# The start of a decoder-trunk kernel written as a table of single steps

## Chip, cores and metric

One core of a Trainium2 chip runs the whole program in one launch. The metric is the time of an execution on the device in microseconds, lower is better. Engines are called as in the profile: PE (TensorE matmuls; PEld its weight loads), DVE (VectorE), ACT (ScalarE), POOL (GpSimd) and SP (the queue that issues most DMAs).

## What is computed

One layer of a hybrid decoder over 1024 prompt tokens and 64 new tokens (1088 columns), width 1024, in float32:

```python
h = rmsnorm(x, g_mix)
z = jnp.einsum('btd,dc->btc', h, w_in)                       # 1024 -> 5 * 512
b_gate, c_gate, v, glu_val, glu_gate = jnp.split(z, 5, axis=-1)
conv_a, new_a = causal_dwconv(c_gate * v, hist_a, conv_a_w)  # 3 taps
y_a = b_gate * conv_a
u_b = glu_val * jax.nn.sigmoid(glu_gate)
conv_b, new_b = causal_dwconv(u_b, hist_b, conv_b_w)         # 31 taps
y_b = jax.nn.silu(layernorm(conv_b + conv_b_bias, ln_b_g, ln_b_b))
x = x + jnp.einsum('btc,cd->btd', jnp.concatenate([y_a, y_b], axis=-1), w_out)
h2 = rmsnorm(x, g_ffn)
f = jax.nn.silu(h2 @ w_gate) * (h2 @ w_up)
x = x + f @ w_down                                           # then a last rmsnorm
```

## The kernel before

Channels lie on the 128 partitions, tokens along the free axis. Every product of two float32 matrices is made of float16 matrices: a value is split into a high half (rounded to float16) and a low half (what is left), and `products` (L217) multiplies high by high, high by low and low by high. So a block of 128 output rows over 8 blocks of the 1024 inputs is 24 matmuls per column range.

The change is in the **first phase**, which makes the norm and the first 4 of the 20 output blocks of the input projection (two gates and two values). There x comes in five chunks of columns (`FIRST`, L57): chunk 0 has 128 columns, chunk 1 has 144, chunks 2, 3 and 4 have 272. For a chunk s and a block k of 128 channels:

- squares: ACT (for half of chunk 0 DVE) squares x, four blocks at a time (`first_squares`, L594);
- halvings: DVE adds the eight blocks of squares in pairs, to one block for chunk 0 and to four for the others (`first_halves`, L605);
- column sums: PE multiplies what is left by a matrix of ones, in float32, and so adds over the partitions (`column_sums`, L251, matmul at L264, output `stat`); the profile counts two rows for each of these matmuls;
- the reciprocal root: two ACT functions and three DVE steps (`rstd_steps`, L271 to L281), the result again in `stat`;
- for each k: DVE multiplies x by the gain and the root into a tile `s` (L637), ACT rounds it to the high half (`high`, L246), DVE subtracts to get the low half (`low`, L249). The low half comes `LAG` = 3 blocks after its tile;
- products: 24 matmuls at L233 for the chunk and an output block, into a PSUM bank `one`.

The four weight blocks are split likewise: high half on ACT (L209), low half on DVE (L210). Gate blocks leave PSUM through a sigmoid on ACT (L667), value blocks through a product on DVE (L514) into the tiles `u` that the 31-tap convolution reads.

The Python text of L681 to L735 is a hand-written order of whole jobs: a chunk's norm, then a block's 24 products, then a chunk's sums, and so on. Each engine executes its instructions strictly in the order in which the text issues them, and waits where an operand isn't ready. So the order of the text is the order of each engine's queue. Among these jobs stand three calls of `fill` (L445), which split the first eight pieces of the weights of the next phase (`raws` 0 and 1); these weights are first scaled on POOL (L196), rounded on ACT (L207) and their low halves made on POOL (L208). `prepare` (L378) loads the next raw block ahead of its use.

After the first phase come the **convolution phase** (from 77.84 us: the other 16 blocks on PE, while DVE runs the 31 taps, L529 and L534), the output projection, and the gated network with a seven-product scheme; DVE makes most of their low halves.

The loads are issued by SP in the order of L310: x chunk 0, weight block 0, x 1, w 1, x 2, w 2, x 3, w 3, x 4.

## Time and profile before

| what | value |
| --- | --- |
| median of 3 runs | 1031.65 us (1030.02 to 1032.03) |
| the profiled execution's own time | 1029.85 us |
| its span, from first to last instruction | 1027.6 us |
| PE busy | 990.8 us (96%) |
| DVE busy | 764.4 us (74%) |
| ACT busy | 390.3 us (38%) |
| POOL busy | 322.6 us (31%) |

The time of the profiled execution holds the span and some 2.3 us around it. A busy share is an average over stages. How much a stage is worth is seen from where PE waits within it: the timeline of an engine lists its instructions in order of time, merged where they are alike, each with its start, the time that the group took, and in brackets the engine's idle time before it with what ended that idle time. A group of matmuls is counted with the pipeline's latency of its last one.

### The profile page before, as it was taken

The numbers are of one execution on the slowest core, as the hardware profiler recorded it, in microseconds if no ns is written. First come the engines' busy times: TensorE is split into PE (matmuls) and PEld (weight loads), VectorE is DVE, ScalarE is ACT, GpSimd is POOL, SyncE is SP. The second block draws the span as 40 slices with busy tenths as digits, with TensorE's granted clock in tenths as the row PEclk, the third lists the DMA queues.
The fourth block names the chain that finished last, engine by engine and source line by source line (L and its number), as shares of the span: only waits on it lengthen the run. The fifth ranks groups of instructions, "written<-read, shape, count | busy, mean of one in ns | idle before, by whom it ended". The sixth has DMA issues, their size and how long they took to land.

```text
span 1027.6 us, 19663 instructions
## 1 busy us (share of the span) xinstructions
PE 990.8 (96%) x8498; PEld 831.2 (81%) x8498; DVE 764.4 (74%) x1083; ACT 390.3 (38%) x694; POOL 322.6 (31%) x259
## 2 busy tenths in 40 slices
PE   4799999999999999999999999999999999999995
PEld 3688888887788878888888888888888888888884
DVE  6839999997687787887776668777676777665548
ACT  6541232335663434444322434332243433233332
POOL 0148764554200013421333332313332322240033
PEclk9899999999999999999999999999999999999998
DMA  9011111211320110111122112011211202111104
GB/s 346 27 42 42 42 42 42 94 42 43 134 83 1 42 42 6 77 42 60 36 72 83 42 41 73 32 35 70 83 42 42 72 32 63 62 63 42 42 1 175
DMA packets 17031, 63.02 MB, mean 61 GB/s; under 512 B 1168, under 2 KB 8480, under 8 KB 12080
## 3 DMA queue, kind: packets, MB, share of 16 engines
q1 hardware_dynamic: 16896, 61.67, 17.3%
q8 instruction: 66, 1.08, 0.4%
q14 instruction: 21, 0.17, 0.1%
q0 software_dynamic: 48, 0.09, 0.0%
HBM read 56.71 MB, written 5.05 MB: 60 GB/s over the span
## 4 chain that ended last, share of the span: by engine, by line
PE 67%; DVE 26%; ACT 3%; issue 2%; DMA 0%; DVEq 0%; ACTq 0%
PE two L233 63%; DVE cv L534 12%; PE one L233 3%; DVE xt L1378 1%; DVE whl L210 1%; DVE u L249 1%; DVE s L637 1%; DVE v L1010 1%; DVE s L281 1%; PE stat L258 1%; DVE h L249 1%; DVE s L280 1%; DVE u L610 1%; DVE cv L529 1%; DVE xt L1326 0%
## 5 line engine op out<-in xcount | busy, mean ns | idle before, releaser
L233 PEld LDWEIGHTS <-whl 128*128 128x128 f16 x7464 | 729.3, 98 | 141.3 <-issue 4.8
L233 PE MATMUL two<-u,whl 128*128 128x272 f16 x4416 | 523.7, 280 | 3.8 <-DVE u L249 2.8
L233 PE MATMUL two<-h,whl 128*128 128x272 f16 x1512 | 186.1, 280 | 0.0
L233 PE MATMUL two<-v,whl 128*128 128x272 f16 x1536 | 178.6, 279 | 0.1
L409 POOL TENSOR_TENSOR s<-wf,s 128x512 f32<-128x512 f32 (+1 forms) x32 | 46.9, 1465 | 383.1 <-DVE whl L210 383.1
L209 ACT ACTIVATE whl<-wf 128x512 f16<-128x512 f32 (+1 forms) x150 | 87.6, 589 | 143.0 <-PE two L233 141.3
L534 DVE SCALAR_TENSOR_TENSOR cv<-u,par_t,cv 128x1024 f32<-128x1024 f32 x116 | 139.7, 1280 | 0.0
L210 DVE SCALAR_TENSOR_TENSOR whl<-wf,whl 128x512 f16<-128x512 f32 (+1 forms) x150 | 108.9, 742 | 1.2 <-ACT whl L209 1.2
L1285 DVE SCALAR_TENSOR_TENSOR xt<-two,xt 128x544 f32<-128x544 f32 x108 | 75.8, 720 | 42.9 <-PE two L233 42.3
L1176 DVE SCALAR_TENSOR_TENSOR s<-two,s 128x544 f32<-128x544 f32 x40 | 28.9, 723 | 66.1 <-PE two L233 66.1
L209 ACT ACTIVATE whl<-s 128x512 f16<-128x512 f32 (+1 forms) x96 | 55.4, 583 | 59.5 <-PE two L233 57.4
L398 POOL TENSOR_TENSOR s<-wf 128x512 f32<-128x512 f32 (+1 forms) x32 | 40.9, 1278 | 108.9 <-DVE u L249 96.3
L210 DVE SCALAR_TENSOR_TENSOR whl<-s,whl 128x512 f16<-128x512 f32 (+1 forms) x96 | 66.6, 708 | 0.0
L208 POOL TENSOR_TENSOR whl<-wf,whl 128x512 f16<-128x512 f32 x38 | 44.1, 1182 | 41.3 <-ACT whl L207 41.3
L233 PE MATMUL two<-u,v 128*128 128x272 f16 x480 | 56.3, 279 | 0.7 <-DVE xt L949 0.7
L233 PEld LDWEIGHTS <-v 128*128 128x128 f16 x480 | 46.9, 98 | 10.0 <-issue 0.9
L246 ACT ACTIVATE h<-s 128x544 f16<-128x544 f32 x52 | 34.0, 657 | 52.8 <-DVE s L1169 48.2
L233 PE MATMUL one<-v,u 128*128 128x272 f16 (+2 forms) x480 | 47.5, 259 | 4.0 <-ACT v L246 2.4
L233 PEld LDWEIGHTS <-u 128*128 128x128 f16 x480 | 40.6, 99 | 11.4 <-issue 5.6
L1210 DVE SCALAR_TENSOR_TENSOR s<-two,s 128x544 f32<-128x544 f32 x20 | 14.5, 724 | 45.2 <-PE two L233 45.2
L405 POOL TENSOR_TENSOR wf<-wf 128x512 f32<-128x512 f32 (+1 forms) x32 | 46.6, 1457 | 0.0
L399 POOL TENSOR_TENSOR s<-s,wf 128x512 f32<-128x512 f32 (+1 forms) x32 | 41.9, 1309 | 2.5
(124 smaller groups left out, 750.9 us busy)
## 6 DMA issues: line engine op xcount, KB each, us to landing
wf<-w_gu SPq DMA_DIRECT2D x22, 1024.0 KB, 4.9
wf<-w_ds SPq DMA_DIRECT2D x12, 768.0 KB, 4.2
wf<-w_in SPq DMA_DIRECT2D x8, 1024.0 KB, 5.0
wf<-w_o SPq DMA_DIRECT2D x6, 1024.0 KB, 4.8
xt<-x SPq DMA_DIRECT2D x3, 1088.0 KB, 10.2
y<-xt SPq DMA_DIRECT2D x2, 1088.0 KB, 4.2
u<-w_in SPq DMA_DIRECT2D x4, 512.0 KB, 8.7
wf<-w_dl SPq DMA_DIRECT2D x2, 1024.0 KB, 5.0
```

The lines of the kernel that those rows point to most:

```text
L208: return whl, lambda: gps.tensor_tensor(lo, wf, hi, ALU.subtract) and None
L209: act.activation(hi, wf, AF.Copy, scale=WSC)
L210: return whl, lambda: dve.scalar_tensor_tensor(lo, wf, WSC, hi, ALU.mult, ALU.subtract) and None
L233: pe.matmul(out, w_[:, wpart, col : col + P], hl[:, apart, t0 : t0 + out.shape[1]], start=first and (i, q) == one, stop=last and (i, q) == ...
L246: act.activation(hi, tmp, AF.Copy)
L398: gps.tensor_tensor(s1, a21, a22, ALU.add)
L399: gps.tensor_tensor(s2, s1, a11, ALU.subtract)
L405: gps.tensor_tensor(a21, a11, a21, ALU.subtract)
L409: gps.tensor_tensor(src, a12, src, ALU.subtract)
L534: dve.scalar_tensor_tensor(o_, i_, w, c, ALU.mult, ALU.add)
L1176: dve.scalar_tensor_tensor(o, src, IN_SC, other, ALU.mult, ALU.add)
L1285: dve.scalar_tensor_tensor(o, bk[a_][:, :, :CW], IN_SC, o, ALU.mult, ALU.add)
```

## The change

The order of the first phase is now a table, `STARTUP`, of single steps; a loop walks it and issues each step. Letters name the step, then come the chunk and the block or part:

- SQ squares; HV a halving on DVE and HP one on POOL; ST one of the matmuls with ones;
- RY and RM the two ACT functions of the root, N its three DVE steps;
- T the normalised tile, HI its high half, LO its low half on DVE, LP its low half on POOL;
- WH and WL a weight block's halves; M half a block's products (12 of 24 matmuls);
- SG the sigmoid, V the product of gate and value;
- FS scaling of the next phase's raw weights, FH and FL the halves of its pieces.

Beside the order, four things differ. Chunks 1 to 4 are halved once more, to two blocks, so that two matmuls with ones are left for each where there were four. Of these eight halvings five stand on POOL (HP10, HP11, HP21, HP40, HP41) and three on DVE (HV20, HV30, HV31); before there were four, all on DVE. Of the 40 low halves 15 stand on POOL. The load of weight block 2 is issued ahead of x's chunk 2. `prepare` no longer loads the raw block 2 of the next phase; it is loaded and scaled at the end of the first phase. The number of products is the same.

```diff
-LAG = 3
+STARTUP = """
+SQ00 SQ01 HV00 WH0 HV01 HV02 ST00 WL0 RY0 RM0 SQ11 N00 N01 SQ10 N02 T06 WH1 HP10 T00 T04 T02
+HI06 T03 HI00 T01 HP11 HI02 T05 HI04 HI03 WL1 HI01 ST10 WH2 ST11 T07 LP00 LO03 LO02 RM1 LO04 RY1
...
+M32h0 FL4 M30h1 SG20 FL1 M31h1 FL6 M33h0 FL3 M23h0 M32h1 SG21 M33h1 V21 V20 M23h1 V11
+"""
 
...
-        ("x", 0), ("w", 0), ("x", 1), ("w", 1), ("x", 2), ("w", 2), ("x", 3), ("w", 3), ("x", 4)
+        ("x", 0), ("w", 0), ("x", 1), ("w", 1), ("w", 2), ("x", 2), ("w", 3), ("x", 3), ("x", 4)
...
-        for q in (r, r + 1):
+        for q in (r, r + 1) if r > 1 else (r,):
...
+    w4, low_w, accs = {}, {}, {}
+    squares_of, left, stat_of, r_of, of_k = {}, {}, {}, {}, {}
+    scaled.update(range(3))
...
+    def first_half(s, level, eng):
+
+        two = squares_of[s, 0]
+        n = 4 >> level
+        other = two[:, n : 2 * n] if level else squares_of.pop((s, 1))
+        eng.tensor_tensor(two[:, :n], two[:, :n], other, ALU.add)
+        left[s] = n
+
+    def first_stat(s, k):
+
+        if k == 0:
+            stat_of[s] = stat_banks()[:, 0, : FIRST[s][1]]
+        n = left[s]
+        pe.matmul(stat_of[s], ones, squares_of[s, 0][:, k], start=k == 0, stop=k == n - 1)
+        if k == n - 1:
+            squares_of.pop((s, 0))
+
...
+        if which == "y":
+            act.activation(
+                y0, st, AF.Abs_reciprocal_sqrt, bias=epst[:, 0:1], scale=1.0 / D
+            )
+        elif which == "m":
+            act.activation(m, st, AF.Identity, bias=epst[:, 0:1], scale=1.0 / D)
...
+    def first_norm(s, k, part):
+
+        hk = h[k][:, :, chunk(s)]
+        if part == "T":
+            t = of_k[s, k] = small()[:, : FIRST[s][1]]
+            dve.scalar_tensor_tensor(
+                t, xt[:, k, chunk(s)], prm(PG1 + k), stat_of[s], ALU.mult, ALU.mult
+            )
+        elif part == "HI":
+            high(hk[:, 0], of_k[s, k])
+        else:
+            low(hk[:, 1], of_k.pop((s, k)), hk[:, 0], gps if part == "LP" else dve)
+
+    def first_task(s, i, part):
         t0, cw = FIRST[s]
         c, o = t0 // CW, t0 % CW
+        if o == 0 and part == 0:
+            accs[c, i] = bank()
+        products(
+            [accs[c, i][:, o : o + cw]],
+            [(w4[i], k * P, [(h[k], t0)]) for k in range(KB)],
+            low_last=s == 0,
+            part=(12 * part, 12 * part + 12),
+        )
...
+    def first_step(step):
+
+        kind = step.rstrip("0123456789h")
+        d = [int(c) for c in step[len(kind) :] if c != "h"]
...
+        elif kind == "WH":
+            w4[d[0]], low_w[d[0]] = split_w(w4f[d[0]], resident=unit)
+        elif kind == "WL":
+            low_w.pop(d[0])()
...
+        elif kind == "FS":
+            r = d[0]
+            if r not in loaded:
+                loaded[r] = load_w(*raws[r][:2])
+            scale_w(loaded[r])
+        elif kind == "FH":
+            fill_one(0)
+            low_w["f", d[0]] = late.pop()
+        elif kind == "FL":
+            low_w.pop(("f", d[0]))()
+
+    keep = {}
+    for step in STARTUP.split():
+        first_step(step)
+    loaded[2] = load_w(*raws[2][:2])
+    scale_w(loaded[2])
```

The queue of POOL at its first tensor work. Before (`wf` a raw weight block, `whl` the halves of its pieces):

```order
L196 TENSOR_SCALAR wf_675<-wf_675 128x2048
L196 TENSOR_SCALAR wf_677<-wf_677 128x2048
L208 TENSOR_TENSOR whl_680<-wf_675,whl_680 128x512
L208 TENSOR_TENSOR whl_683<-wf_675,whl_683 128x512
L208 TENSOR_TENSOR whl_790<-wf_675,whl_790 128x512
L208 TENSOR_TENSOR whl_792<-wf_675,whl_792 128x512
```

With the change (`u` squares, `v` the halves of the normalised x, `s` the normalised tiles; L627 is a halving, L263 a low half):

```order
L627 TENSOR_TENSOR u_138<-u_138,u_134 128x576
L627 TENSOR_TENSOR u_138<-u_138 128x288
L263 TENSOR_TENSOR v_101<-s_146,v_101 128x128
L263 TENSOR_TENSOR v_108<-s_171,v_108 128x128
L263 TENSOR_TENSOR v_103<-s_206,v_103 128x144
L627 TENSOR_TENSOR u_204<-u_204 128x544
L263 TENSOR_TENSOR v_101<-s_251,v_101 128x144
L263 TENSOR_TENSOR v_102<-s_273,v_102 128x144
L627 TENSOR_TENSOR u_381<-u_381,u_352 128x1088
L627 TENSOR_TENSOR u_381<-u_381 128x544
L210 TENSOR_SCALAR wf_524<-wf_524 128x2048
```

Two halvings of chunk 1 now head the queue, and ten steps of the norm stand ahead of the first scaling.

The queue of PE at its start. Before (`stat` column sums, `one` an output block; `v_101` to `v_108` are the blocks k = 0 to 7 of the normalised x):

```order
L264 MATMUL stat_129<-u_119,ones 128x128
L233 LDWEIGHTS u_126
L233 MATMUL one_176<-v_101,u_126 128x128
...
L233 MATMUL one_176<-v_106,u_126 128x128
L264 MATMUL stat_189<-u_134,ones 128x144 x4
L233 LDWEIGHTS u_126
L233 MATMUL one_176<-v_107,u_126 128x128
```

With the change:

```order
L635 MATMUL stat_128<-u_119,ones 128x128
L635 MATMUL stat_166<-u_138,ones 128x144 x2
L247 LDWEIGHTS u_124
L247 MATMUL one_190<-v_101,u_124 128x128
L247 LDWEIGHTS u_124
L247 MATMUL one_190<-v_101,u_124 128x128
```

Chunk 1's sums stood behind the first 12 products, four matmuls long; they now stand ahead of all products, two matmuls long.

The queue of DVE where chunk 2 is normalised. Before (the last step of the root, tiles, a halving of chunk 3, then tiles and low halves in turn):

```order
L281 SCALAR_TENSOR_TENSOR stat_279<-u_308 128x272
L637 SCALAR_TENSOR_TENSOR s_341<-xt,par_t,stat_279 128x272
L637 SCALAR_TENSOR_TENSOR s_344<-xt,par_t,stat_279 128x272
L637 SCALAR_TENSOR_TENSOR s_347<-xt,par_t,stat_279 128x272
L610 TENSOR_TENSOR u_230<-u_230,u_244 128x1088
L637 SCALAR_TENSOR_TENSOR s_351<-xt,par_t,stat_279 128x272
L249 TENSOR_TENSOR v_101<-s_341,v_101 128x272
L637 SCALAR_TENSOR_TENSOR s_355<-xt,par_t,stat_279 128x272
L249 TENSOR_TENSOR v_102<-s_344,v_102 128x272
```

With the change:

```order
L627 TENSOR_TENSOR u_275<-u_275 128x544
L664 SCALAR_TENSOR_TENSOR s_398<-xt,par_t,stat_306 128x272
L664 SCALAR_TENSOR_TENSOR s_413<-xt,par_t,stat_306 128x272
L664 SCALAR_TENSOR_TENSOR s_415<-xt,par_t,stat_306 128x272
...
L664 SCALAR_TENSOR_TENSOR s_455<-xt,par_t,stat_306 128x272
L664 SCALAR_TENSOR_TENSOR s_458<-xt,par_t,stat_306 128x272
L263 TENSOR_TENSOR v_102<-s_432,v_102 128x272
L263 TENSOR_TENSOR v_105<-s_415,v_105 128x272
L263 TENSOR_TENSOR v_101<-s_435,v_101 128x272
```

All eight tiles now stand ahead of the first low half, the halvings of chunk 3 ahead of the tiles, and the low half of block 0, which the second product of the chunk reads, is the third of them.

## Rows read from the trace of the kernel before

**Rows 1.** Page, part 4: the chain that ended last, by line.

```profile
PE two L233 63%; DVE cv L534 12%; PE one L233 3%; DVE xt L1378 1%; DVE whl L210 1%; DVE u L249 1%; DVE s L637 1%; DVE v L1010 1%; DVE s L281 1%; PE stat L258 1%; DVE h L249 1%; DVE s L280 1%; DVE u L610 1%; DVE cv L529 1%; DVE xt L1326 0%
```

**Rows 2.** Timeline of PE to 140 us: start, us, engine, line, instructions, idle before.

```profile
7.62 0.76 PE L264 MATMUL stat<-u,ones 128*128 128x128 f32 x2 [7.62 <-DVE u L614]
10.80 0.26 PE L233 MATMUL one<-v,u 128*128 128x128 f16 x1 [2.42 <-ACT v L246]
...
14.22 2.20 PE L264 MATMUL stat<-u,ones 128*128 128x144 f32 x8
...
20.35 2.10 PE L264 MATMUL stat<-u,ones 128*128 128x272 f32 x8 [1.92 <-DVE u L610]
22.29 5.12 PE L233 MATMUL one<-v,u 128*128 128x144 f16 x72
32.68 4.00 PE L264 MATMUL stat<-u,ones 128*128 128x272 f32 x8 [5.27 <-DVE u L610]
36.47 7.42 PE L233 MATMUL one<-v,u 128*128 128x144 f16 x96
45.33 2.10 PE L264 MATMUL stat<-u,ones 128*128 128x272 f32 x8 [1.44 <-DVE u L610]
47.27 30.74 PE L233 MATMUL one<-v,u 128*128 128x272 f16 x264
77.84 62.37 PE L233 MATMUL two<-v,whl 128*128 128x272 f16 x537
```

**Rows 3.** Windows: length, busy us (x) of five engines, PEclk, DMA share, GB/s.

```profile
10.80:16.30 5.50, 4.10 (x21) 3.20 (x21) 4.93 (x16) 3.80 (x9) 0.00 (x0) 1.00 1.09 382
...
32.60:36.70 4.10, 4.02 (x10) 2.92 (x11) 4.10 (x12) 3.09 (x7) 0.00 (x0) 0.50 0.00 0
```

**Rows 4.** Timeline of ACT to 90 us.

```profile
8.93 1.25 ACT L600 ACTIVATE u<-xt 128x576 f32<-128x576 f32 x2
...
14.63 1.09 ACT L600 ACTIVATE u<-xt 128x1088 f32<-128x1088 f32 x1
```

**Rows 5.** Timeline of DVE to 90 us.

```profile
10.06 1.12 DVE L637 SCALAR_TENSOR_TENSOR s<-xt,par_t,stat 128x128 f32<-128x128 f32 x4
...
14.97 1.22 DVE L210 SCALAR_TENSOR_TENSOR u<-u,u 128x1024 f16<-128x1024 f32 x1
...
18.18 0.91 DVE L637 SCALAR_TENSOR_TENSOR s<-xt,par_t,stat 128x144 f32<-128x144 f32 x3
19.02 1.28 DVE L610 TENSOR_TENSOR u<-u,u 128x1088 f32<-128x1088 f32 x1
...
22.47 0.74 DVE L249 TENSOR_TENSOR v<-s,v 128x144 f16<-128x144 f32 x3
...
26.65 2.13 DVE L279 SCALAR_TENSOR_TENSOR u<-u 128x272 f32<-128x272 f32 x1
...
29.77 1.31 DVE L637 SCALAR_TENSOR_TENSOR s<-xt,par_t,stat 128x272 f32<-128x272 f32 x3
...
36.00 1.49 DVE L249 TENSOR_TENSOR v<-s,v 128x272 f16<-128x272 f32 x4
...
41.33 0.43 DVE L279 SCALAR_TENSOR_TENSOR u<-u 128x272 f32<-128x272 f32 x1
...
78.73 2.59 DVE L529 TENSOR_SCALAR cv<-u,par_t 128x1024 f32<-128x1024 f32 x2
```

**Rows 6.** Timeline of POOL to 110 us.

```profile
25.85 2.64 POOL L196 TENSOR_SCALAR wf<-wf 128x2048 f32<-128x2048 f32 x1 [23.63 <-DMA wf<-w_in]
29.57 1.92 POOL L196 TENSOR_SCALAR wf<-wf 128x2048 f32<-128x2048 f32 x1 [1.08 <-DMA wf<-w_in]
```

**Rows 7.** POOL by line and shape: busy us, mean ns of one, idle before.

```profile
L208 POOL TENSOR_TENSOR whl<-wf,whl 128x512 f16<-128x512 f32 x38 | 44.1, 1182 | 41.3 <-ACT whl L207 41.3
...
L558 POOL TENSOR_TENSOR u<-u 128x512 f32<-128x512 f32 x4 | 5.1, 1269 | 0.3
```

More of the change, by code (lines that the diff above doesn't have):

```diff
@@ L590, in trunk, with chunk @@
         new_u()
[L591 to L594 removed]
+    w4, low_w, accs = {}, {}, {}
+    squares_of, left, stat_of, r_of, of_k = {}, {}, {}, {}, {}
+    scaled.update(range(3))
+    def chunk(s):
         t0, cw = FIRST[s]
[L597 to L603 removed]
@@ L605, in first_halves @@
-    def first_halves(s, n):
-        two = squares_of[s]
-        m = 4
-        if n < 8:
-            dve.tensor_tensor(two[0], two[0], two[1], ALU.add)
-            two.pop()
-        while m > n:
-            m //= 2
-            dve.tensor_tensor(two[0][:, :m], two[0][:, :m], two[0][:, m : 2 * m], ALU.add)
-        squares_of[s] = [t[:, k] for t in two for k in range(m)]
-    def first_stat(s):
-        stat_of[s] = column_sums(squares_of.pop(s))
-    def first_rstd(s):
-        if s not in stat_of:
-            first_stat(s)
-        three = unit([P, 3, FIRST[s][1]])
-        st = stat_of.pop(s)
-        r_of[s] = rstd_steps(st, 1.0 / D, ASC, [three[:, i] for i in range(3)] + [st])
@@ L629, in first_norm @@
-    def first_norm(s, **beside):
-        t0, cw = FIRST[s]
-        r = r_of[s]()
-        ts = []
-        for k in range(KB + LAG):
-            if k < KB:
-                t = small()[:, :cw]
-                dve.scalar_tensor_tensor(
-                    t, xt[:, k, t0 : t0 + cw], prm(PG1 + k), r, ALU.mult, ALU.mult
-                )
-                high(h[k][:, 0, t0 : t0 + cw], t)
-                ts.append(t)
-            if f"k{k}" in beside:
-                beside[f"k{k}"]()
-            if k >= LAG:
-                hk = h[k - LAG][:, :, t0 : t0 + cw]
-                low(hk[:, 1], ts[k - LAG], hk[:, 0])
@@ L648, in first_task, with first_squares @@
-    def first_task(s, *blocks):
+        return slice(t0, t0 + cw)
+    def first_squares(s, i):
+        o = squares_of[s, i] = unit([P, 4, FIRST[s][1]])
+        xi = xt[:, 4 * i : 4 * i + 4, chunk(s)]
+        if (s, i) == (0, 1):
+            dve.tensor_tensor(o, xi, xi, ALU.mult)
+        else:
+            act.activation(o, xi, AF.Square)
+    def first_half(s, level, eng):
[4 more added lines that the diff above has]
+        left[s] = n
@@ new lines, in first_stat, with first_rstd @@
+    def first_stat(s, k):
[5 more added lines that the diff above has]
+            squares_of.pop((s, 0))
+    def first_rstd(s, which):
+        st = stat_of[s]
+        if s not in r_of:
+            three = unit([P, 3, FIRST[s][1]])
+            r_of[s] = [three[:, i] for i in range(3)]
+        y0, m, t1 = r_of[s]
+        if which == "y":
[4 more added lines that the diff above has]
+            act.activation(m, st, AF.Identity, bias=epst[:, 0:1], scale=1.0 / D)
+        elif which == 0:
+            dve.scalar_tensor_tensor(t1, m, -0.5 * ASC, y0, ALU.mult, ALU.mult)
+        elif which == 1:
+            dve.tensor_tensor(t1, t1, y0, ALU.mult)
+        else:
+            dve.scalar_tensor_tensor(st, t1, 1.5 * ASC, y0, ALU.add, ALU.mult)
@@ L649, in first_task @@
+    def first_norm(s, k, part):
[7 more added lines that the diff above has]
+            high(hk[:, 0], of_k[s, k])
+        else:
+            low(hk[:, 1], of_k.pop((s, k)), hk[:, 0], gps if part == "LP" else dve)
+    def first_task(s, i, part):
         t0, cw = FIRST[s]
@@ L650, in first_task @@
         c, o = t0 // CW, t0 % CW
-        for i in blocks:
-            if o == 0:
-                accs[c, i] = bank()
-            products(
-                [accs[c, i][:, o : o + cw]],
-                [(w4[i], k * P, [(h[k], t0)]) for k in range(KB)],
-                low_last=s == 0,
-            )
-    def first_w(i):
-        w, fn = split_w(w4f[i], resident=unit)
-        w4.append(w)
-        return fn
-    def first_gate(c, j):
-        sg = small()[:, :CW]
-        act.activation(sg, accs[c, 2 * j][:, :CW], AF.Sigmoid, scale=IN_SC)
-        return sg
```

104 lines of the change are left out of this document (32 added, 72 removed).

## The prediction

> **What bounds the kernel now.** I read the chain of waits first, then the timeline of PE, then the other engines over the stretch where PE has gaps. The chain [rows 1] is PE for the most part; a tenth of it is the 31-tap convolution on DVE. PE has nearly all its idle time in the first 47 us, and that is the stretch the change rewrites [rows 2]: 7.62 us until the first column sum, 2.42 to the first product, then 1.92, 5.27 and 1.44 us, each ahead of a chunk's column sums and each ended by a halving on DVE (L610). From 47.27 us PE doesn't wait again in the first phase: 264 products of 272 columns take 30.74 us, 0.1164 us each, and the next phase follows at 77.84 us. So the end of the first phase is **the moment from which PE waits no more, plus the products that are then left**. Before: 47.27 + 30.74, less 0.2 us of pipeline at the end, gives 77.84.
>
> What comes after is the same code and moves with it: DVE's taps begin at 78.73 us [rows 5], 0.9 us behind PE, because they wait for the last value block, which PE ends. DVE is on the chain there, but it starts earlier by as much as PE does.
>
> **The first product.** It moves back. Chunk 1's column sums now stand ahead of all products, and their halvings are on GpSimd. ACT ends chunk 1's squares at 8.93 + 1.25 = 10.2 us [rows 4]. A GpSimd addition of 512 elements takes 1.27 us [rows 7], so 576 take 1.43 and 288 some 0.72 by proportion: 12.4 us. Two matmuls with ones are half of the 2.20 us group at 14.22 us [rows 2], about 1.0. First product at 13.4 us, against 10.80: 2.6 us lost there.
>
> **PE's own work until chunk 2.** The first 12 products follow DVE's low halves of chunk 0 (eight tiles, weight block 1's low half, then the lows), which by the steps below are done at 15.8 us. Then 180 products of 128 or 144 columns stand in the queue, of all four weight blocks, where before each block came with its own wait. 72 such products took 5.12 us [rows 2], so 180 take 12.6: 28.4 us. The sums of chunks 2, 3 and 4 are two matmuls each, half of 2.10 us: 3.1 in all, 31.5 us, if their halvings are ready. That removes half of five groups' time on PE, and with it the slow one: the group at 32.68 us took 4.00 us, not 2.10, at a granted clock of 0.50 [rows 3], which is 1.2 GHz, after PE had stood idle for 5.27 us. In the new order I see no wait of over 2 us behind the first product, so those 1.9 us go as well.
>
> **DVE until chunk 2 is ready.** Back to back, an instruction starts about 0.07 us before the last one ends: the three tiles at 18.18 us are followed at 19.02 [rows 5]. By the groups in those rows a step is 0.26 us for a tile of 128 columns, 0.28 for 144, 0.41 for 272; 0.22 for a low half of 144 and, as the nearest, of 128; 0.36 for one of 272; 1.15 for a weight block's low half; 1.21 for a first halving of 272 columns, for the second, half as long, 0.65; 0.36 for a step of the root on 272 columns and about 0.26 on 144. From the first tile at 10.06 us, which doesn't move, the table puts on DVE ahead of chunk 2's first low half: 8 + 8 + 8 tiles (2.1 + 2.2 + 3.3), three weight blocks (3.5), 6 and 5 low halves (1.3 + 1.1), six root steps (1.9), three halvings (3.1). That is 18.5 us, so 28.6 us. The third low half of chunk 2 is that of block 0, which the chunk's second product reads; three of them take 1.1: 29.7 us without any collision.
>
> **The collisions.** In the trace a DVE step that reads two SBUF tiles and a GpSimd tensor step do not run at once. The root step at 26.65 us took 2.13 us, where its twin at 41.33 took 0.43 [rows 5], and it ends 0.3 us after the GpSimd scaling that began at 25.85 [rows 6]. That scaling itself took 2.64 us against 1.92 for the next, having begun under a DVE step. Tiles read the root from PSUM and so only one SBUF tile. The change puts ten GpSimd steps of the norm and one scaling into these 32 us. By walking both queues I find three meetings before 28.6 us (weight block 1 with a halving, a root step and weight block 3 with low halves), 0.8 us together; and one large one: GpSimd ends the last halving of chunk 4 at about 29.6 us and goes straight on to scale the next phase's raw weights, landed since 25.85, just when DVE begins chunk 2's low halves. Two of those go behind it: 1.9 us. Sum: 29.7 + 0.8 + 1.9 = 32.4 us. Bounds: no collision, and PE's own 31.5 us decides; or all eleven steps (11.1 us by proportion to rows 7, and the 1.92) stop DVE fully, which gives 40.8. I take 32.4, as the only large meeting of the trace cost 1.7 us.
>
> The Trainium skill has this as a rule (SBUF — State Buffer, "Who interferes with whom"): a DVE instruction with two SBUF inputs and a GpSimd instruction that reads SBUF exclude each other for the whole instruction, whoever starts first. The trace agrees, with the 2.13 us. The rule speaks against moving low halves to GpSimd, and without it the sum would be by some 0.9 us better, no more, since PE's own work is next.
>
> **From there on.** 288 products of 272 columns are left, 33.5 us at 0.1164: 65.9 us. Their operands come in time: chunk 4 is due on PE 6 x 12 products later, at 40.8 us, and the tightest, a low half on GpSimd due at about 44, is ready by my walk some 0.7 us earlier. I add 0.4 us for small waits: **66.3 us, 11.5 us ahead of 77.84**.
>
> What costs nothing: weight block 2 ahead of x's chunk 2 delays that chunk by 512 KB, 1.4 us at 382 GB/s [rows 3]; it was first squared at 14.63 us, by an ACT that hadn't idled for it [rows 4], and in the new order ACT, with three weight and chunk steps ahead, comes to it, by a walk like the ones above, at 14.8. If that cover fails it costs at most those 1.4. The rest of the low halves on GpSimd (chunks 3 and 4) lies beside DVE tiles. The raw weights' low halves now end GpSimd's queue: seven at 1.18 us [rows 7] after about 53 us, so 61.5; only then can raw block 2 be loaded, but eight tasks of 48 products come ahead of its first use, 44.7 us.
>
> **The sum.** The profiled execution took 1029.85 us: 1029.85 - 11.5 = 1018.3. The median of the runs shown, 1031.65, lies 1.8 above that execution; from it the result would be 1020.1. I forecast between them, **1019.2 us**.
>
> **Rivals.**
>
> *Collisions weigh more.* More GpSimd steps meet DVE than my walk shows. I counted 2.7 of 11.1 us; were it twice that, the result is 2.7 later, 1022; with all of it, 1028. For it: eleven steps now run where two did, and the timing of meetings isn't mine to choose. Against it: the tiles, the longest part of DVE's work there, don't collide, and the table puts GpSimd's long halvings beside them. Chance 0.13.
>
> *GpSimd isn't ready (slower than before).* All products now stand behind two GpSimd halvings wanted at 10.2 us. Before, GpSimd did no tensor work until 25.85 us, after 23.63 us idle [rows 6]; nothing shows that it could have. If its first step is late, chunk 1's sums, all products and all that follows are late by as much: 15.6 us if it were not ready before 25.85, so 1034.8. The change becomes a loss once that first step starts after 21.7 us. Against it: at 25.85 it began when its data landed, and its extra 0.7 us is explained by the DVE step. Chance 0.05. The Trainium skill (GPSIMD Engine Reference, 2.1 Instruction dispatch) gives the first call of a freshly loaded GpSimd kernel about 6 us more; by that the result, as an estimate, would be 1025. No run here shows it.
>
> *The clock.* PE starts at the lower level in any case: at 14.22 us 8 matmuls of 144 columns took as long as 8 of 272 do at 20.35 [rows 2]. If it rises later than before, or falls again at the new wait near 31 us, the price lies between nothing and that of the slow stretch doubled, 3.8; with 1.9 the result is 1021. For it: the first product is later, and the first dozen is sparse. Chance 0.07.
>
> *The gain is lost downstream.* If DVE's tap phase, on the chain, had a bound of its own in time, PE would meet it and give back the 11.5: 1031, no change. Against it: every instruction of that phase is the same and its start hangs on PE. Chance 0.03.
>
> **The numbers.** Forecast 0.72, then 0.13, 0.05, 0.07, 0.03. A measurement tells about 0.2%, 2 us, from no change. Faster: the forecast, the clock, nearly all of the collisions, part of the GpSimd case: 0.93; same 0.03; slower 0.04. The range reaches down to the case without collisions against the profiled execution (1018.3 - 1.3 and as much for the scatter of runs: 1016) and up to doubled collisions with the clock's share and the scatter of the runs (1022 + 1.9 + 1): 1025.
>
> **What would show it.** Right: first product near 13.4 us; no PE gap over 2 us after it; the last wait near 32 us, ended by a DVE low half that lies beside GpSimd's scaling; the next phase at 66 us; clock 1.00 from then on; the taps 0.9 us behind. Wrong: a first GpSimd halving that starts later than 10.5 us or takes far over 1.5; PE waits between 35 and 60 us; a phase that starts at 66 and an end that hasn't moved.

## Result, and the profile after

The changed kernel takes **1019.45 us** (median of 4 runs, 1019.09 to 1020.71) beside 1031.06 us for the kernel before on the same chip: ratio 0.989, 95% interval 0.9873 to 0.9907. The forecast was 1019.2 us, range 1016 to 1025. The profiled execution took 1019.75 us, its span is 1018.0 us, 9.6 less than before; by the sum against the profiled execution it should have been 1018.3. By the spans, 9.6 us of the expected 11.5 came: 0.8 of the missing 1.9 us are lost in the first phase, 1.1 some 190 us later. The time of the execution shows only 1.4 us of this, because it holds 1.75 us beside the span here and held 2.25 before.

The timeline of PE in the changed kernel, to be laid beside [rows 2] (start, us, engine, line, instructions, idle before):

```profile
7.45 0.77 PE L635 MATMUL stat<-u,ones 128*128 128x128 f32 x2 [7.45 <-DVE u L627]
12.43 1.33 PE L635 MATMUL stat<-u,ones 128*128 128x144 f32 x4 [4.21 <-POOL u L627]
13.55 0.61 PE L247 MATMUL one<-v,u 128*128 128x128 f16 x3
14.58 7.57 PE L247 MATMUL one<-v,u 128*128 128x128 f16 x81 [0.41 <-DVE v L263]
21.98 0.68 PE L635 MATMUL stat<-u,ones 128*128 128x272 f32 x2
...
23.68 4.66 PE L247 MATMUL one<-v,u 128*128 128x144 f16 x72
...
31.10 1.18 PE L635 MATMUL stat<-u,ones 128*128 128x272 f32 x4 [0.24 <-POOL u L627]
32.12 0.28 PE L247 MATMUL one<-v,u 128*128 128x272 f16 x1
33.80 33.53 PE L247 MATMUL one<-v,u 128*128 128x272 f16 x287 [1.39 <-DVE v L263]
67.17 5.03 PE L247 MATMUL two<-v,whl 128*128 128x272 f16 x42
```

The three long gaps of before, 1.92, 5.27 and 1.44 us, are gone; one of 1.39 us is new. The first product starts at 13.55 us (forecast 13.4), PE's own work reaches the 272-column products at 32.1 (31.5), the last wait ends at 33.80 (32.4), and the next phase starts at 67.17 (66.3) where it was 77.84. Now POOL's queue, with the halvings (L627), low halves (L263) and the scaling (L210):

```profile
10.11 1.40 POOL L627 TENSOR_TENSOR u<-u,u 128x576 f32<-128x576 f32 x1 [7.89 <-ACT u L620]
...
29.71 1.34 POOL L627 TENSOR_TENSOR u<-u 128x544 f32<-128x544 f32 x1
31.02 2.08 POOL L210 TENSOR_SCALAR wf<-wf 128x2048 f32<-128x2048 f32 x1
```

POOL's first halving starts as soon as ACT's squares are there and takes 1.40 us, against 1.43 estimated. And DVE around chunk 2, with the taps behind the phase:

```profile
24.84 0.44 DVE L653 SCALAR_TENSOR_TENSOR u<-u 128x272 f32<-128x272 f32 x1 [1.47 <-ACT u L647]
...
27.20 3.35 DVE L664 SCALAR_TENSOR_TENSOR s<-xt,par_t,stat 128x272 f32<-128x272 f32 x8
30.46 4.69 DVE L263 TENSOR_TENSOR v<-s,v 128x272 f16<-128x272 f32 x7
67.85 2.60 DVE L543 TENSOR_SCALAR cv<-u,par_t 128x1024 f32<-128x1024 f32 x2
```

Two things stand out. DVE is idle for 1.47 us before chunk 2's root, which the forecast's walk did not have. And the seven low halves take 4.69 us, not 7 x 0.36: the scaling on POOL lies beside them, as forecast. Most of the excess is in one of the seven, which took 2.12 us where the median is 0.43 (duration ns min/median/max, then first and last start):

```profile
L263 DVE TENSOR_TENSOR v<-s,v x7: 427/429/2123, 30.5 to 34.7; 128x272 f16<-128x272 f32 x7
```

ACT, which releases DVE there, waited for PE itself:

```profile
23.94 0.49 ACT L651 ACTIVATE u<-stat,epst 128x272 f32<-128x272 f32 x1 [1.43 <-PE stat L635]
```

PE was late because the 81 products ahead of chunk 2's sums took 7.57 us, 0.093 us each, where 72 of 144 columns took 5.12, 0.071 each [rows 2]. One group of instructions by stretch shows how, in two executions whose first phase is the same code: the changed kernel up to 20.3 us and behind it,

```profile
L247 PE MATMUL one<-v,u x34: 287/314/314, 16.7 to 20.2; 128*128 128x128 f16 x34
...
L247 PE MATMUL one<-v,u x42: 219/219/287, 20.2 to 23.1; 128*128 128x128 f16 x42
```

and experiment 9, which edits only what comes 180 us later:

```profile
L247 PE MATMUL one<-v,u x29: 266/314/314, 14.7 to 17.9; 128*128 128x128 f16 x29
...
L247 PE MATMUL one<-v,u x52: 219/219/277, 17.9 to 20.8; 128*128 128x128 f16 x52
```

There DVE's idle time ahead of the same root is short:

```profile
23.76 0.44 DVE L657 SCALAR_TENSOR_TENSOR u<-u 128x272 f32<-128x272 f32 x1 [0.28 <-ACT u L651]
```

A product takes 314 ns while the granted clock is at the lower level (1.2 GHz) and 219 ns at the upper one (2.4 GHz), pipeline included. In one execution the change of level came at 20.4 us, in the other at 18.0; before, it was at 16.3. (The column of the granted clock says 1.00 ahead of the first change that a trace has, so at the start of a run the level must be read from durations.) "Full clock from" in the table below is that moment.

Behind the first phase 1.1 us more of the span went. The chain of waits there reads (start, us, what):

```profile
255.82 2.50 POOL v L222
258.34 5.93 DMA wf<-w_o
264.35 1.06 ACT v L223
265.44 1.42 DVE v L224 x2
```

and PE behind it:

```profile
268.48 10.12 PE L247 MATMUL two<-u,v 128*128 128x272 f16 x86 [1.88 <-DVE xt L942]
```

A load of 1 MB of the output weights starts when POOL frees its buffer, lands 5.93 us later, ACT rounds it, DVE makes its low halves, and only then, because it stands behind them in the queue, comes DVE's first eviction (L942) of the output projection, for which PE waits 1.88 us. In the kernel before the same wait was 0.69 us: there the load landed 4.74 us after its issue, just ahead of the end of products on PE, and it is these that ended ACT's idle time (5.51 us, to 274.03). In both traces and in those of runs 1 to 8 PE's wait is the landing time of this load less some 4.05 us.

### The profile page after: what moved, and what is told of

It reads as the page before. It is cut to its first block, busy times and chain, and to the rows that moved or that the text cites. A ratio compares the mean times of both kernels' runs of the same rounds, so it can differ in the third digit from the quotient of the medians.

```text
span 1018.0 us, 19624 instructions
## 1 busy us (share of the span) xinstructions
PE 986.4 (97%) x8482; PEld 829.8 (82%) x8482; DVE 761.1 (75%) x1067; ACT 385.8 (38%) x692; POOL 340.6 (33%) x279
## 4 chain that ended last, share of the span: by engine, by line
PE 68%; DVE 25%; ACT 3%; issue 2%; DMA 1%; POOL 0%; DVEq 0%; ACTq 0%
PE two L247 63%; DVE cv L548 12%; PE one L247 4%; DVE xt L1371 1%; DVE whl L224 1%; DVE u L263 1%; DVE v L1003 1%; DMA wf<-w_o 1%; DVE s L295 1%; PE stat L272 1%; DVE h L263 1%; DVE s L294 1%; DVE cv L543 1%; DVE v L263 1%; DVE xt L1319 0%
## 5 line engine op out<-in xcount | busy, mean ns | idle before, releaser
L224 DVE SCALAR_TENSOR_TENSOR whl<-wf,whl 128x512 f16<-128x512 f32 (+1 forms) x150 | 112.3, 765 | 1.2 <-ACT whl L223 1.2
L247 PEld LDWEIGHTS <-u 128*128 128x128 f16 x480 | 42.8, 104 | 8.7 <-issue 2.6
L222 POOL TENSOR_TENSOR whl<-wf,whl 128x512 f16<-128x512 f32 x38 | 44.1, 1187 | 10.1 <-ACT whl L221 10.0
```

Of the source, the lines that this page charges most:

```text
L222: return whl, lambda: gps.tensor_tensor(lo, wf, hi, ALU.subtract) and None
L224: return whl, lambda: dve.scalar_tensor_tensor(lo, wf, WSC, hi, ALU.mult, ALU.subtract) and None
L247: pe.matmul(out, w_[:, wpart, col : col + P], hl[:, apart, t0 : t0 + out.shape[1]], start=first and (i, q) == one, stop=last and (i, q) == ...
```

## Experiments

The kernel before ran beside them, with medians of 1031.54 us (beside 1 to 4), 1031.53 (5 to 8), 1030.07 (9 and 10) and 1030.18 (11 and 12); the ratios are against these. Its runs lie in two groups some 1.7 us apart (below, under the median), and these medians fall into one or the other, so the ratios of 9 to 12 stand some 0.0014 higher than those of 1 to 8 for that alone. "272 from" is the start of the 272-column products after the last wait ahead of them; "xt" is PE's wait for DVE's first eviction near 268 us. The first column sums, whose code is the same in runs 1 to 11, start between 7.12 and 7.76 us, so a place in the trace carries 0.6 us of scatter from there beside that of the clock.

| run | full clock from | 272 from | next phase | xt | median us | ratio, 95% interval |
| --- | --- | --- | --- | --- | --- | --- |
| changed kernel | 20.4 | 33.80 | 67.17 | 1.9 | 1019.45 | 0.9890, 0.9873 to 0.9907 |
| 1 again | 20.0 | 33.80 | 67.17 | 1.4 | 1020.70 | 0.9903, 0.9887 to 0.9918 |
| 2 order alone | 22.8 | 36.18 | 69.93 | 0.9 | 1023.55 | 0.9926, 0.9911 to 0.9941 |
| 3 lows on DVE | 20.7 | 34.04 | 68.95 | 2.7 | 1022.83 | 0.9916, 0.9896 to 0.9937 |
| 4 halvings on DVE | 18.8 | 32.66 | 66.16 | 2.2 | 1022.55 | 0.9917, 0.9893 to 0.9941 |
| 5 scaling later | 19.8 | 31.84 | 66.29 | 2.0 | 1019.35 | 0.9886, 0.9870 to 0.9902 |
| 6 ones between | 17.7 | 32.39 | 65.76 | 0.8 | 1017.54 | 0.9877, 0.9859 to 0.9895 |
| 7 four ones | 17.6 | 32.99 | 66.49 | 0.9 | 1019.95 | 0.9894, 0.9875 to 0.9913 |
| 8 old load order | 19.8 | 34.22 | 67.59 | 2.4 | 1021.05 | 0.9908, 0.9892 to 0.9923 |
| 9 evictions first | 18.0 | 32.73 | 66.10 | 0 | 1019.10 | 0.9890, 0.9873 to 0.9906 |
| 10 three edits | 19.9 | 31.89 | 66.35 | 0 | 1017.51 | 0.9876, 0.9861 to 0.9891 |
| 11 two edits | 20.5 | 32.18 | 66.63 | 0 | 1018.26 | 0.9884, 0.9869 to 0.9898 |
| 12 ones from the start | 22.3 | 33.39 | 67.84 | 0 | 1017.73 | 0.9873, 0.9857 to 0.9890 |

**1. The changed kernel again**, no edit.

> The changed kernel once more, with nothing edited. Theory: of the 10.7 us that the next phase starts earlier (67.17 us instead of 77.84), 1.2 us were lost again in the profiled execution behind one load of output weights that took 5.9 us to land (issued at 258.34), where in the kernel before it took 4.7; that is scatter of one load, so this profile should show the next phase at 67.2 us give or take 1, and from there to the end of the span 949.6 to 951 us, by the length of that load. Rival: the new order makes that load or its consumer late; then the loss of 1.2 us behind it comes back each time.

The first sums started 0.31 us later and the clock rose 0.35 us earlier; from the sums of chunk 2 on (21.98 us in both) the first phase is the same within 0.02 us. The load took 5.41 us, PE waited 1.35 us for it, and 950.3 us followed the first phase. The median is 1.25 us higher. So differences between medians of about 1 us are scatter, and small edits are judged by the place in the trace. Whether the new order itself makes that load longer stays open: it took 4.82 us or more in all nine traces of it up to run 8, but the kernel before has one trace only.

**2. The order alone.** In the table, and in the loads:

```diff
- HP.. LP..   (steps on POOL)
+ HV.. LO..   (the same steps on DVE)
- HV11 HV21 HV31 HV41
+ ST12 ST13 ST22 ST23 ST32 ST33 ST42 ST43
-        ("x", 0), ("w", 0), ("x", 1), ("w", 1), ("w", 2), ("x", 2), ("w", 3), ("x", 3), ("x", 4)
+        ("x", 0), ("w", 0), ("x", 1), ("w", 1), ("x", 2), ("w", 2), ("x", 3), ("w", 3), ("x", 4)
```

> The table's order kept, all else undone: no halving and no low half on GpSimd, four matmuls with ones a chunk, x's chunk 2 loaded ahead of weight block 2. Theory (the order is the gain): the next phase starts at 69 to 71 us, since PE still finds the 180 products of chunks 0 and 1 together in its queue, DVE's 15 low halves and one level of halving are mostly beside PE's work, and no collision is left; result 1021 to 1023. Rival (taking work off DVE is the gain): DVE gets back about 4.9 us of low halves and 2.9 us of halvings less the second level, PE four more pairs of matmuls with ones, 4 us; the next phase starts at 75 us or later, result 1027 or more.

```profile
34.30 2.05 PE L635 MATMUL stat<-u,ones 128*128 128x272 f32 x8
36.18 9.31 PE L247 MATMUL one<-v,u 128*128 128x272 f16 x79
...
69.93 2.25 PE L247 MATMUL two<-v,whl 128*128 128x272 f16 x18
```

PE has no wait between 16.89 and 36.18 us: its own work, with the longer sums and the latest clock rise, decides. The median is 8.0 us below the kernel before, where run 1, beside the same runs of the kernel before, is 10.8 below. **Most of the gain is the order of the queues**, before any step is moved to another engine. (The later load of raw block 2 also stays in this run.) How the other 2.8 us of the phase divide isn't shown: part of them is this run's late clock rise.

**3 and 4. One kind of step back on DVE**: all low halves (`LP` to `LO`), or all halvings (`HP` to `HV`).

> One part undone: all 40 low halves on DVE, the halvings stay on GpSimd. Theory: the low halves of chunks 3 and 4 lie beside PE's 33 us of work and cost nothing; of chunks 0 and 1 five come back to DVE ahead of chunk 2 (about 1.1 us), less the 0.5 to 0.8 us of collisions that go; next phase at 67.2 to 68.5 us. Rival (work off DVE is the gain): fifteen low halves of 0.22 to 0.36 us come back, 4.9 us; 71 to 72 us.

> One part undone: all halvings on DVE, the low halves stay on GpSimd. Theory: chunk 1's first halving lies on DVE ahead of weight block 1 and lets the first product start about 0.8 us earlier (0.75 + 0.4 us on DVE in place of 1.40 + 0.79 on GpSimd), but DVE's way to chunk 2's low halves gets longer by 0.7 + 0.4 + 0.65 + 1.2 + 0.65 = 3.6 us less the collisions of the halvings and, as the scaling then runs earlier beside the tiles, less the 1.7 us behind it; next phase at 68 to 69.5 us. Rival (the halvings on GpSimd are the gain): 71 us or later.

With the low halves on DVE the last wait ends 0.24 us later than in the changed kernel. The phase start is 1.8 later, but a stretch at the lower clock stands in the 287 products, which took 35.07 us and not 33.53 (window: length, then busy us of five engines, granted clock 0.50):

```profile
34.40:37.60 3.20, 3.20 (x16) 2.13 (x14) 3.16 (x9) 0.73 (x2) 0.00 (x0) 0.50 0.03 5
```

Without that, 67.4: the low end of the expectation, and the move of the low halves is worth 0.2 us there, which is within the scatter of the start. With the halvings on DVE the expectation missed: chunk 1's sums come no later (12.30 against 12.43 us), and the next phase starts earlier than in the changed kernel:

```profile
31.64 1.18 PE L635 MATMUL stat<-u,ones 128*128 128x272 f32 x4 [1.57 <-DVE s L664]
32.66 33.66 PE L247 MATMUL one<-v,u 128*128 128x272 f16 x288
```

Without POOL's halvings ahead of it the scaling moved to 26.9 us and off DVE's low halves, which took 2.54 us for seven. Its earlier clock rise helped, too; but run 9, with the halvings on POOL and the rise at 18.0 us, reached the 272-column products at 32.73, no earlier. So the halvings on POOL bring nothing that shows to this phase by themselves. The medians of 3 and 4 are some 2 us above that of run 1, with intervals that overlap; part is the waits for xt of 2.7 and 2.2 us and further stretches at the lower clock (below).

**5. The scaling later.**

```diff
- ... M21h0 FS0 T45 T40 V00 HI40 M20h1 T47 SG01 T43 T41 LP40 FH0 T44 M22h0 SG10 FL0 T42 HI43 HI41 HI42 M21h1 FH1 V10 HI47 LO41 HI45 N31
+ ... M21h0 T45 T40 V00 HI40 M20h1 T47 SG01 T43 T41 LP40 FS0 T44 M22h0 SG10 T42 HI43 HI41 HI42 M21h1 V10 HI47 LO41 HI45 FH0 FL0 FH1 N31
```

> GpSimd's scaling of the next phase's first raw weights goes behind its low half of chunk 4, its high and low halves behind a later high half; the same steps, nothing else moved. Theory (the scaling is what held chunk 2's low halves on DVE): in the changed kernel seven of them took 4.69 us from 30.46 us on, where 7 x 0.36 would be 2.5, and PE's last wait ended at 33.80 us though its own work was done at 32.3. Without the scaling beside them the 287 products begin at 32.3 to 32.6 us and the next phase at 65.8 to 66.3 us, 0.9 to 1.4 ahead of 67.17; the time is lower by as much, about 1 us, within the scatter of the runs (the place in the trace decides). Rival (any GpSimd step in that place holds DVE as long; the low half of chunk 4 moves up and takes the scaling's part): the last wait stays at 33.5 us or later and the next phase at 67 us. Second rival (the raw weights' scaling was placed early because the next phase needs it): the next phase starts no earlier, with a wait for a high half ahead of its first product.

```profile
30.18 3.00 DVE L263 TENSOR_TENSOR v<-s,v 128x272 f16<-128x272 f32 x7
```

```profile
L263 DVE TENSOR_TENSOR v<-s,v x7: 427/429/889, 30.2 to 32.7; 128x272 f16<-128x272 f32 x7
```

```profile
31.84 9.31 PE L247 MATMUL one<-v,u 128*128 128x272 f16 x79
41.58 0.51 PE L247 MATMUL one<-v,u 128*128 128x272 f16 x3 [0.43 <-DVE v L263]
42.43 24.02 PE L247 MATMUL one<-v,u 128*128 128x272 f16 x206 [0.35 <-DVE v L263]
```

The theory holds: the low halves take 1.7 us less, the wait of 1.39 us is gone. Half of it comes back at 41.6 and 42.4 us, where POOL's steps now meet low halves of chunk 4; the phase starts 0.88 us earlier. The Trainium skill (SBUF — State Buffer, "Who interferes with whom") calls the ports that DVE and GpSimd share an exclusive lock, held for a whole instruction. The trace agrees: beside the scaling, which took 2.08 us, one low half took 2.12; here, beside the end of a halving on POOL only, the longest took 0.89, and in run 4, beside no POOL step, all seven took 0.43.

**6. Ones between.** Eight matmuls of the ones matrix with itself fill PE's gap behind the first sums; their output is overwritten.

```diff
- ... ST00 WL0 ...
+ ... ST00 D08 WL0 ...
+        if kind == "D":
+            ...
+                pe.matmul(accs[0, 0][:, :P], ones, ones, start=True, stop=True)
```

> Eight more matmuls of the ones matrix with itself (128 columns, float32) are put on PE behind chunk 0's column sums, where it stands idle from 8.2 to 12.4 us; they write into the first block's bank, whose first product clears it, so the output is the same. By the pair of such matmuls at 7.45 us (0.77 us) they take 3.1 us and end by 11.4, so nothing is late for them. Theory (the clock's late rise is the mis-sized term: the products of chunks 0 and 1 ran until 20.37 us at the lower level, and what the chip grants depends on what PE did before): the rise comes earlier than 20 us, the 81 products of the second stretch take less than 7.57 us, and the next phase starts 0.7 to 1.5 us earlier, at 65.7 to 66.5. Rival (the rise doesn't answer to work in that gap): it comes between 18.8 and 22.8 us as in the four traces of the new order so far, and the next phase starts at 67.2. Second rival (PE's earlier end of the first products is no use, since DVE's low halves of chunk 2 end last): the rise is earlier, but the last wait still ends at 33.8 us and is only longer than 1.39 us; the next phase stays at 67.2.

The clock was high from 10.9 to 14.3 us and again from 17.7; the 81 products took 6.38 us, chunk 2's sums came at 20.57, DVE's idle time ahead of its root fell from 1.47 to 0.33, the last wait ended at 32.39 and the next phase started at 65.76. So an earlier rise does reach the end of the phase, through PE's sums and DVE. Whether the ones caused it this run cannot say, as runs 9 and 10 showed afterwards.

**7. Four ones**: steps `HV..1`/`HP..1` out, `ST.2` and `ST.3` in, for chunks 1 to 4.

> The second halving of chunks 1 to 4 is left out again (its steps are gone from the table) and their column sums are four matmuls with ones each instead of two; the rest of the table stands. Theory (PE's own work was 32.3 us and lies close behind DVE's): four chunks' sums take two more matmuls each, half of 2.10 us, of which chunk 2's, 3's and 4's and in part chunk 1's lie ahead of the 272-column products, 3.1 to 4.1 us more on PE, at the lower clock level for the first ones; GpSimd and DVE are rid of five halvings of 0.65 to 0.72 us. PE then decides alone: the products begin at about 34 to 35.5 us, the last wait on a low half is gone, and the next phase starts at 67.8 to 69 us; time 0.6 to 2 us above the changed kernel. Rival (DVE decides and gains by the halvings it and GpSimd are rid of): the next phase at 66.5 us or earlier. Second rival (chunk 1's sums come earlier without the second GpSimd halving, so all products begin 0.7 us earlier and this pays for the matmuls): next phase at 67.2, no change.

The last wait on a low half is gone, as expected, but the theory missed the time: chunk 1's sums are longer (2.29 against 1.33 us) but start at 11.30 and not 12.43, the clock rises at 17.6, the products begin at 32.99 and the next phase at 66.49, the first rival's figure with the help of the early rise. The median is 0.5 us above the changed kernel's. The second halving and the shorter sums pay for each other.

**8. The old load order** (the loads' line of run 2, alone).

> x's chunk 2 is loaded ahead of weight block 2 again, as before the change; nothing else moved. Theory (the order of these two loads costs and brings next to nothing): weight block 2 lands 1.5 us later and chunk 2 1.4 us earlier; in the changed kernel DVE takes weight block 2's low half some microseconds after it has landed, and ACT comes to chunk 2 only at about 14.8 us. The next phase starts between 66.9 and 68 us, the time is that of the changed kernel within 0.1%. Rival (the block's high half is what ACT's queue stands behind): ACT waits for weight block 2 and all behind it, chunk 2's squares among it, is up to 1.5 us later; the next phase at 68 to 69 us and a time 1 to 1.5 us higher. Second rival (chunk 2's earlier landing helps): next phase at 66.5 us or before.

```profile
14.12 1.06 ACT L223 ACTIVATE u<-u 128x1024 f16<-128x1024 f32 x1 [2.07 <-DMA u<-w_in]
15.09 0.36 ACT L651 ACTIVATE u<-stat,epst 128x144 f32<-128x144 f32 x1
```

The edit moves two blocks, not one: the changed kernel loads weight block 3 ahead of x's chunk 3, too, and this run puts both back. The size is the theory's, the mechanism the rival's: ACT waits 2.07 us for weight block 2 and comes to chunk 1's root at 15.09 instead of 13.80 us; DVE waits 1.46 us for that. For weight block 3 ACT waits 0.30 us, at 18.41. Much of it is absorbed, and the phase starts 0.42 us later than in the changed kernel. Beside run 5, whose clock rose at the same 19.8 us and whose code is the changed kernel's up to there, the sums of chunk 2 come 0.7 us later (22.40 for 21.70).

**9. Evictions first.** The last pair of the output projection's resident weight blocks is split six tasks later.

```diff
-        if res and t < marks["out"] or not res and len(live) == NSLOT:
+        if res and t < marks["out"] + (6 if e_last(i) else 0) or not res and len(live) == NSLOT:
```

> The last pair of w_o's resident blocks is split six tasks later, behind the first evictions of the out projection; the first phase is left as the changed kernel has it. Theory (the 1.2 us that the changed kernel gave back behind the first phase were lost there: DVE's low halves of that pair stood ahead of its first eviction (L942), they waited for ACT's high halves, and those for a load of 1 MB that took 5.93 us instead of 4.74, so that PE waited 1.88 us for xt instead of 0.69): in the new order DVE evicts as PE ends each block, PE's wait for xt is gone or under 0.4 us, and from the next phase's start to the end of the span it takes 949 to 950 us instead of 950.8 and 950.3 in the two traces of the changed kernel; the median is 1 to 2 us lower, 1018 to 1019, and the runs lie closer together. Rival (the loads behind that pair now start some 10 us later and are late themselves): a new wait of PE for the weights of the out projection's second half or of the next products between 300 and 340 us, and no gain. Second rival (PE's wait is bound by something else, as the 0.69 us of the kernel before): a wait of about 0.7 us for xt stays.

```profile
265.35 10.12 PE L247 MATMUL two<-u,v 128*128 128x272 f16 x86
```

```profile
369.60:372.90 3.30, 3.30 (x15) 2.16 (x15) 3.12 (x5) 0.00 (x0) 0.00 (x0) 0.50 0.00 0
```

The wait is gone. From 66.10 us to the end it still took 950.8 us, because a stretch at the lower clock fell at 369.6 us; in runs 10, 11 and 12, without one, it took 949.0, 949.1 and 949.0, where the changed kernel took 950.8 and 950.3. So the wait's share is 1.3 to 1.8 us, and the four runs lie within 0.8 us of each other. This first phase is unedited, and yet the next phase starts at 66.10, not 67.17; what differs in the trace is the clock's rise, at 18.0 instead of 20.4 us.

**10 and 11. Edits 5, 6 and 9 together, and 5 and 9 without the ones.**

> The three edits together: the scaling behind GpSimd's low half of chunk 4, the eight matmuls of ones behind chunk 0's column sums, the last pair of w_o's resident blocks split after the first evictions. Theory (late clock, late last low halves and the coupled eviction are three separate losses): PE's own work ends about 30.7 us as in the run with the ones, no low half holds it, so the 288 products begin at 30.3 to 31 us and the next phase at 64.0 to 65.0 us; with 949 to 950 us behind it the span is 1013 to 1015 and the time 1015 to 1017 us, some 3 us below the changed kernel and 15 below the kernel before. Rival (the first two are one loss, DVE's): the next phase starts at 65.7 us as with the ones alone, and the time is 1016.5 to 1018. Second rival (with PE earlier, the low halves of chunks 2 and 4 are now what it meets): new waits of PE between 32 and 45 us that sum to 1 us or more; the next phase again at 65.5 us or later.

> The kernel of the three edits without the matmuls of ones: only the scaling later and w_o's last pair split after the first evictions. It tells whether the ones had any part in that kernel's 1017.5 us. Theory (they had none: with them the granted clock rose at 19.9 us in one execution and at 17.7 in another, while the untouched first phase of the kernel with the evictions first showed 18.0): clock rise somewhere between 17.5 and 21 us, PE's own work ends at 30.5 to 32 us, the next phase starts at 65.2 to 66.6 us, the median is within 0.6 us of 1017.5. Rival (the ones do bring the rise forward on average, by about 1 us): the median is 1018.2 or more.

Run 10 missed its 64 to 65 us: the ones were there, the clock rose only at 19.9, and the first phase is that of run 5. In its trace 0.8 us of the gain over the changed kernel lie in the first phase and 1.9 behind it, where the wait for xt is gone. Run 11 rose at 20.5; its median is 0.75 us above, which meets the rival's figure (1018.2 or more) by 0.06 us and so, with medians that scatter by 1 us, decides nothing. The ones after the first sums are not shown to do anything.

**12. Ones from the start**: 14 ahead of the first sums and 9 behind them.

> The kernel of the three edits with PE kept at work from the first microsecond: 14 matmuls of ones with themselves ahead of the first column sums and 9 behind them (by the 3.62 us that eight took, 6.3 and 4.1 us at the lower level), so PE stands idle for under 2 us in all before the first product at 13.5 us. Theory (the granted clock rises some time after PE has begun to work without pauses, and before the change that was after the first products): the rise comes before 13 us, the 81 products take 5.8 us (at 0.071 us each, as 72 took 5.12 before) instead of 7.3, PE's own work ends at 29.2 to 30.5 us, and the next phase starts at 64.0 to 65.3 us; the median is 1015.2 to 1016.8. Rival (float32 matmuls of ones do not raise it, as in the run of the three edits): rise at 17.5 us or later, next phase at 65.5 to 66.5, median at 1017.5. Second rival (the first column sums stand behind the ones and come late): first sums after 7.8 us, first product after 13.8, and no gain at the end.

```profile
1.04 5.39 PE L696 MATMUL one<-ones 128*128 128x128 f32 x28 [1.04 <-POOL ones L311]
...
7.49 2.17 PE L696 MATMUL one<-ones 128*128 128x128 f32 x18
13.08 1.33 PE L639 MATMUL stat<-u,ones 128*128 128x144 f32 x4 [3.42 <-POOL u L631]
...
16.34 7.07 PE L247 MATMUL one<-v,u 128*128 128x128 f16 x73 [0.74 <-DVE v L263]
```

```profile
5.30:12.00 6.70, 3.62 (x30) 3.24 (x29) 6.31 (x16) 5.38 (x14) 2.14 (x2) 1.00 1.04 363
12.10:22.30 10.20, 8.48 (x72) 8.21 (x73) 9.08 (x23) 7.89 (x15) 5.51 (x7) 0.50 1.10 383
```

Half of the theory holds: continuous work raised the clock at 5.3 us. But at the upper level the second group of ones took 2.17 us, not 4.1; PE then stood idle for 3.42 us, the clock fell at 12.1 and came back only at 22.3, later than in any run but one, and the next phase began at 67.84. The median, 1017.73 us, is the rival's figure. The other three executions took 1016.23 to 1018.19 us; what their clocks did in the first phase is not recorded. Enough ones to fill the gap at the upper level were not tried.

## Why the prediction was right, and where it was off

**First product**: right (13.55 for 13.4), and so was POOL's readiness. The Trainium skill (GPSIMD Engine Reference, 2.1 Instruction dispatch) gives the first call of a freshly loaded kernel about 6 us more. Nothing like it appeared in POOL's first halving, 1.40 us; whether its code was freshly loaded no row tells.

**PE's own work and DVE's walk until chunk 2**: here a step failed. "72 such products took 5.12 us, so 180 take 12.6" priced products at the upper clock that ran in part at the lower one, until 20.4 us: the first sums of chunk 2 stood on PE until 21.98. PE's own end came only 0.6 us late because the products behind, at the upper level, cost less than priced (4.66 us for the 72 of 144 columns, not 5.12). And "DVE until chunk 2 is ready" ran DVE back to back and left out that its root waits for PE's sums, the first of which stands behind 84 of those products. The 1.47 us of idle time there are the 1.4 by which the last wait ended late (33.80 for 32.4). When the level rose at 18.0 us, in run 9, the same code lost 0.28 us there, and the wait ended at 32.73, close to the forecast. (These are two executions and not an experiment on the clock: no edit was shown to bring this rise forward.) The clock was listed as a rival with 0 to 3.8 us; it belonged into the sum.

**The collisions**: right in place and size. The large one was priced at 1.9 us; seven low halves took 2.2 more than 7 x 0.36, and run 5 took 1.7 of it away; the rest is the halving that ran ahead of the scaling.

**The loads**: the prediction weighed weight block 2 ahead of x's chunk 2 and left out that block 3 moved ahead of chunk 3 as well. Neither cost anything in the changed kernel: ACT came to chunk 2 at 14.74 us (14.8 by the walk) and waited for no load there. By run 8 the new order even pays 0.4 to 0.7 us, because it keeps ACT from a wait for block 2.

**From there on**: 288 products took the forecast 33.5 us; the 0.4 us for small waits was not needed. So the next phase starts 10.67 us earlier instead of 11.5.

**Downstream**: "what comes after is the same code and moves with it" is true but for 1.1 us, and not at the tap phase, which the rival named: DVE's first eviction of the output projection stands behind a load, whose landing took 4.7 to 6.7 us in these traces. DVE's taps start 0.7 us behind PE, for a forecast of 0.9.

**The median**: 11.6 us below that of the kernel before, where the two profiled executions are 10.1 us apart, their spans 9.6 and their next phases 10.67. So part of the 11.6 is where the median before fell, between two runs at 1030.0 and 1030.5 us and two at 1031.7 and 1032.0. That 1019.2 came so near to 1019.45 is partly luck: the forecast was put halfway between two starting points 1.8 us apart, and the eight runs of the changed kernel, run 1 included, spread over 1019.1 to 1022.4. What the kernel before scatters by has a candidate: all its 28 runs beside the experiments lie at 1029.75 to 1030.36 us with a mean granted clock of 0.993 to 0.996, or at 1031.5 to 1032.0 with 0.991 to 0.992. That fits one stretch at the lower clock of the price below, but those executions have no trace.

Of the parts of the change, then: the listed order brings about 8 of some 11 us; the rest is that of the engine moves, the second halving and the load order together, and of run 2's later clock rise. Taken singly no trace shows more than 0.4 us lost to the changed kernel without one of them (3, 4, 7, 8), or 0.7 for the load order at an equal clock. What part of the order brings the 8 was not taken apart. Of what was tried, runs 6, 10 and 12 have the lowest medians, within 0.2 us of each other and some 2 us below the changed kernel.

## What to carry to other kernels

Where one engine's queue is rewritten, walk the queues together: an engine that looks back to back can wait for a sum that stands behind another engine's bulk work, and that work must be priced at the clock it will have. A good order of the same steps can be worth more than moving steps to an idle engine, and an idle engine that shares something with the busy one gives part of it back. When variants differ by a microsecond, compare a place in the trace, and look for what scatters (a load, a clock level) before naming a cause.

## What the runs showed of the hardware

The moment at which PE's clock rises moved between 18.0 and 20.4 us in three executions of one and the same first phase (the changed kernel, runs 1 and 9), and came at 19.8 and 20.5 in runs 5 and 11, whose first edit comes later. Between the 18.0 and the 20.4 the end of the phase moved by 1.1 us. What sets the moment is open.

Later, too, short stretches at the lower level appeared in some executions, shortly behind waits of PE of 1.4 to 2.4 us, near 34, 268 and 370 to 376 us, and not in others with the same code there: in the changed kernel none followed waits of 1.39, 1.88 and 1.58 us at these places. One adds 1.5 to 1.7 us of matmul time: 35.07 us for 33.53 in run 3, and in run 4 the 86 products at 268 us, at a granted clock of 0.50 to 271.4, against the 10.12 us of the same 86 in the changed kernel above. PE's next wait can take up part of it: the one of 0.57 us ahead of the column sums near 279 us in the changed kernel is gone in run 4.

```profile
267.81 11.79 PE L247 MATMUL two<-u,v 128*128 128x272 f16 x86 [2.24 <-DVE xt L942]
```

The 1 MB load of w_o ahead of the first eviction took 4.74 us to land in the kernel before, 5.93 in the changed one, and 5.41, 4.91, 6.74, 6.29, 6.10, 4.82, 4.91 and 6.45 in runs 1 to 8, with the same code around it. What makes it slower is open.
